# Norm2 and the gate operands by token quarters inside the output projection; down weights first, and first and last down pairs with the inner tile outermost

## The chip, the cores and the metric

The kernel runs on one core of one Trainium2 chip. Its engines are TensorE (PE, matmuls; PEld is its weight load), VectorE (DVE), ScalarE (ACT), GpSimd (POOL) and SyncE (SP), whose queue issues every DMA of this kernel. The metric is the device time of one execution in microseconds, the median of the runs of a kernel. A profile is one execution; its span goes from the first to the last instruction.

## The reference

One encoder layer, for a prompt of 1024 tokens and a sample of 32, which the kernel holds side by side as T = 1056 columns. What matters here is its second half:

```python
    m = jax.nn.sigmoid(ga_br) * y_a + jax.nn.sigmoid(gb_br) * y_b
    x = x + gate1 * (m @ w_out)

    h2 = _rms_norm(x, norm2_g) * (1 + scale2) + shift2
    g, up = jnp.split(h2 @ w_gate_up, 2, axis=-1)
    x = x + gate2 * ((jax.nn.silu(g) * up) @ w_down)
```

All is float32. D_MODEL is 1024 (8 tiles of 128), D_FF is 2816 (22 tiles). The shifts, scales and gates come from a conditioning vector, one for the prompt and one for the sample.

## The kernel before

**Precision.** Each float32 operand is split in two parts that TensorE takes: `split` (L81 to L83) writes a rounded copy (the high part, an ACT cast, L82) and the difference to it (the low part, a subtraction on VectorE, L83). A product is three matmuls: high by high, high by low, low by high.

**Output projection (L885 to L907).** `m` lies in `oh` and `ol`, all 1056 columns. For each of the 8 output tiles `n`, `wpiece` loads 512 KB of weights through a staging buffer `st` (`stage`, two buffers, shared by all loads of this half) and splits them into two of the seven `ws` buffers. `out_unit` (L818) runs 24 matmuls into one of six PSUM buffers `u`, adds gate and residual on VectorE (L815), and adds the square to `ssq` (ACT L829, DVE L830). The residual itself comes by `residual_in` (L786): a load through `st`, eight transposes on PE into a PSUM buffer `x` (two of them), two copies. The tiles 0 to 4 run over three groups of 352 columns. The last three have their weights held, and run over four quarters of QW = 264 columns: first quarters 0 and 2 for each tile, then 1 and 3.

**Norm2 and operands.** Gate and up projection use a Strassen scheme with seven products. It is run for two token groups: group 0 pairs quarters 0 and 2, group 1 quarters 1 and 3. `norm2(g)` (L832) sums the squares over the partitions with 128x1 matmuls (L839), takes the power -1/2 (DVE L841, POOL L842), spreads the result over the partitions with matmuls against the identity (L850), multiplies (DVE L854) and modulates (ACT L857). This gives four blocks of 4 x 264 columns per group, b11, b12 (both upper four tiles; first and second quarter) and b21, b22. `operands` (L863) forms from them, in place, B11, T1 = b12 - b11, T2 = b22 - T1, T3 = b22 - b12, B22, T4 = b21 - T2 and B21, each split in two; the low part of B21 on POOL. `norm2(0)` starts behind the second of the six last output units, its second part behind the fourth; `operands(0)` stands behind the last unit.

**Gate-up (L1019 to L1049).** Per pair of tiles `f0` and for gate (`uw` 0) and up (`uw` 1), `wstrassen` forms seven weight operands, which fill the seven `ws` buffers, and `strassen` (L951) runs seven products of 12 matmuls per group. They take the operands in the order B11, T2, T1, B21, T3, B22, T4 (`SEQ`, L917). The first gate pass is run for group 0 alone, with `norm2(1)` hooked in behind its products 1 and 4; then comes `operands(1)`, then the same pass for group 1. All other passes run both groups. The result of each tile is stored to `a_d`. The 14 operands lie in three places: four in `Ta`, free from the start; eight in `Tb`, where `oh` and `ol` were; two in the place of `xb`.

**Down projection (L1053 to L1138).** The 22 tiles of the inner dimension are taken in two halves of 11 (`KC`). `a_load` (L991) brings one tile of `a_d` through `st` and splits it into one of 11 places: two (`k0`, `k1`) loaded early, nine where the Strassen operands were, which come free as the last gate-up pass moves on. Three more places (`late`) take the first three tiles of the second half. `x1_load` brings the residual `x1` back, eight loads of 528 KB. `d_piece` loads the weights of one output tile, 1408 rows, in two loads, and fills three `ws` buffers. In each half the output tiles 0 and 1 are a pair with the inner tile outermost: 18 matmuls per inner tile into six PSUM buffers. Tiles 2 to 5 follow one by one, then 6 and 7, three column groups each. Behind the first half the eight places left are loaded anew. In the second half the outputs are transposed and stored on the way.

**What sets the order.** PE runs in the order of the lines. The order on ACT, DVE, POOL and SP is made when the kernel is built, by a scheduler that knows the dependencies and the buffers; each engine then runs its own queue strictly in that order, and a waiting instruction holds up what is queued behind it. So a DMA of x1 (L909) can stand in the middle of the output projection though its line is behind it.

Of the kernel before, what the change touches and what calls it, by code (L numbers as in the profile page):

```python
# [7 lines left out]
F32 = mybir.dt.float32  # L8
# [30 lines left out]
def hybrid_layer(tc, x_prompt, x_sample, cache_k, cache_v, state_conv, c_prompt, c_sample,  # L39
# [726 lines left out]
    OPS = ("B11", "T1", "T2", "B21", "T3", "B22", "T4")  # L766
# [10 lines left out]
    Ta = sb("Ta", side="right")  # L777
    Dp = sb("Dp", side="right")
# [53 lines left out]
    def norm2(g):  # L832

        qs = (g * QW, g * QW + HW)
        starts = (0, P, QW - P)
        pm = x_tile()
        for j, q in enumerate(qs):
            for i, c in enumerate(starts):
                pe.matmul(pm[:, 3 * j + i:3 * j + i + 1], ssq[:, q + c:q + c + P], ones[:, 0:1], start=True, stop=True)  # L839
        rs = Dp.tile([P, 6], F32, tag="rs2", name="rs2", bufs=2)  # L840
        dve.tensor_scalar(out=rs, in0=pm[:, 0:6], scalar1=EPS, scalar2=None, op0=ALU.add)  # L841
        pool.tensor_tensor(out=rs, in0=rs, in1=mhalf[:, :6], op=ALU.pow)  # L842

        def rest():
            b = {}
            for j, q in enumerate(qs):
                pr = x_tile()
                for i, c in enumerate(starts):
                    c0 = i * P - c
                    pe.matmul(pr[:, c + c0:c + P], rs[:, 3 * j + i:3 * j + i + 1].to_broadcast([P, P]), ident[:, c0:],  # L850
                              start=True, stop=True)
                for i, x in enumerate((xa, xb)):
                    h2 = Dq.tile([P, 4, QW], F32, tag=f"h2{i}{j}", name="h2", bufs=1)
                    dve.tensor_mul(h2, x[:, :, q:q + QW], pr[:, :QW].unsqueeze(1).to_broadcast([P, 4, QW]))  # L854
                    for n in range(4):
                        for c0, c1, s in pieces(q, QW):
                            act.activation(h2[:, n, c0:c1], h2[:, n, c0:c1], AF.Identity,  # L857
                                           scale=a2[:, 4 * i + n, s:s + 1], bias=mod[:, 3 * KT + 4 * i + n, s:s + 1])
                    b[i, j] = h2
            return b  # L860
        return rest

    def operands(g, b):  # L863

        def parts(o, src, eng=dve):
            split(src, Top[o, g][:, 0], Top[o, g][:, 1], eng)

        b11, b12, b21, b22 = b[0, 0], b[0, 1], b[1, 0], b[1, 1]
        parts("B11", b11)
        dve.tensor_sub(b11, b12, b11)  # L870
        t1 = b11
        parts("B22", b22)
        dve.tensor_sub(b12, b22, b12)
        t3 = b12
        dve.tensor_sub(b22, b22, t1)
        t2 = b22
        parts("T2", t2)
        parts("T1", t1)
        parts("B21", b21, pool)
        dve.tensor_sub(b21, b21, t2)  # L880
        t4 = b21
        parts("T3", t3)
        parts("T4", t4)

    for n in range(KT - 3):  # L885
# [8 lines left out]
    LAST = tuple(range(KT - 3, KT))  # L894
    w3 = [wpiece(wo_v[:, :, n * P:(n + 1) * P]) for n in LAST]
    alloc_ops(Ta, order[:NTA])
    for n, w_ in zip(LAST, w3):
        for j, q in enumerate((0, 2)):
            out_unit(n, w_, q * QW, QW, (lambda n=n: residual_in(n)) if j == 0 else None)
    todo = [(n, w_, q) for n, w_ in zip(LAST, w3) for q in (1, 3)]  # L900
    blocks = []
    for i, (n, w_, q) in enumerate(todo):
        out_unit(n, w_, q * QW, QW)
        if i == 1:
            stat = norm2(0)
        if i == 3:
            blocks.append(stat())  # L907
# [259 lines left out]
```

## Time and profile before

| | |
|---|---|
| median of 3 runs | 2210.89 us (2209.64 to 2211.85) |
| the profiled execution | 2211.65 us |
| its span | 2209.9 us |
| mean granted TensorE clock | 0.970 |
| PE busy | 2066.9 us (94%) |
| DVE, ACT, POOL busy | 1218.1, 771.9, 391.3 us |
| DMA | 206.93 MB, mean 94 GB/s |

Every matmul record has a length that overlaps the next one, so PE's time is read from counts per stretch and from the idle times before a group of matmuls. An arrow "<-" names what ended an idle time: the engine and line, or the DMA, that released it. PEclk is the clock that was granted to TensorE, as a share of full speed. In the text the stretches of the span are given in microseconds from its start: the output projection ends at 1386.5, the gate-up stage at 1883.6, the first half of the down projection at 2042.

### The profile page before, as it was taken

To read this page: it belongs to the slowest core of one execution; us is meant where nothing else is said; L and a number is where in the kernel's file an instruction comes from. 1 tells how busy PE (TensorE), PEld (TensorE's weight loads), DVE (VectorE), ACT (ScalarE), POOL (GpSimd) and SP (SyncE) were. 2 spreads that over 40 slices of the span, in tenths; PEclk is the share of its full clock that TensorE was granted. 3 is DMA by queue.
4 is the path that set the end of the run, shared out by engine and by line. 5 is a ranking of instruction groups with operands and counts; after the bars stand their busy time and mean duration, and the time that the engine had idled before them with its cause. 6 is when DMAs were issued, how large, how long until landed. Compare 5 with 4: busy or idle time off the path is not lost.

```text
span 2209.9 us, 36054 instructions
## 1 busy us (share of the span) xinstructions
PE 2066.9 (94%) x13931; PEld 2018.9 (91%) x13931; DVE 1218.1 (55%) x2770; ACT 771.9 (35%) x1875; POOL 391.3 (18%) x644
## 2 busy tenths in 40 slices
PE   7899999999999999999999999589999999599699
PEld 5899998989999999999999999489999999599598
DVE  5665656565656556555576845665555555222232
ACT  5354545444444444322221222633333333111210
POOL 2333333333333232000000000111211211000000
PEclk9999999999999999999999999689999999799799
DMA  9211212021212010546586533112322324512321
GB/s 263 76 55 49 67 38 79 21 82 30 75 30 73 28 45 17 148 155 186 164 258 200 166 97 118 37 59 78 94 72 74 92 69 119 189 40 79 104 67 55
DMA packets 286195, 206.93 MB, mean 94 GB/s; under 512 B 12976, under 2 KB 269768, under 8 KB 286024
## 3 DMA queue, kind: packets, MB, share of 16 engines
q1 hardware_dynamic: 286024, 204.63, 30.6%
q8 instruction: 110, 1.80, 0.3%
q14 instruction: 61, 0.50, 0.1%
HBM read 153.74 MB, written 50.84 MB: 93 GB/s over the span
## 4 chain that ended last, share of the span: by engine, by line
PE 59%; DVE 3%; DMA 3%; ACT 2%; issue 1%; POOL 1%; SPq 0%; ACTq 0%; DVEq 0%; POOLq 0%
PE u L970 17%; PE u L689 7%; PE u L687 7%; PE u L688 7%; PE u L1087 4%; PE u L1089 4%; PE u L1088 4%; DMA st<-a_d 1%; PE mm L526 1%; DMA st<-in_w_down_dram 1%; PE mm L527 1%; PE mm L528 1%; PE mm L485 1%; PE mm L487 1%; PE mm L486 1%
## 5 line engine op out<-in xcount | busy, mean ns | idle before, releaser
L82 ACT CAST ws<-st 128x512 fp32r<-128x512 f32 (+1 forms) x282 | 170.5, 614 | 503.8 <-PE u L1089 122.8
L83 DVE TENSOR_TENSOR ws<-st,ws 128x512 fp32r<-128x512 f32 (+1 forms) x260 | 181.5, 704 | 293.9 <-ACT ws L82 292.3
L970 PE MATMUL u<-T,ws 128*128 128x264 f32 x1848 | 240.7, 287 | 19.6 <-ACT T L82 14.7
L970 PEld LDWEIGHTS u<-T,ws 128*128 128x128 f32 x1848 | 232.9, 191 | 21.1 <-ACT T L82 15.3
L1087 PE MATMUL u<-ka,ws 128*128 128x352 f32 x480 | 159.4, 332 | 49.9 <-ACT ws L82 49.9
L526 PE MATMUL mm<-hh,wh 128*128 128x352 f32 x576 | 198.4, 344 | 0.0
L970 PE MATMUL u<-B,ws 128*128 128x264 f32 x1320 | 174.7, 286 | 15.5 <-ACT B L82 14.1
L528 PE MATMUL mm<-hh,wl 128*128 128x352 f32 x576 | 188.1, 327 | 0.0
L527 PE MATMUL mm<-hl,wh 128*128 128x352 f32 x576 | 187.9, 326 | 0.0
L485 PE MATMUL mm<-qh,hh 128*128 128x384 f32 x512 | 183.8, 359 | 3.0 <-ACT hh L82 2.9
L970 PEld LDWEIGHTS u<-B,ws 128*128 128x128 f32 x1320 | 167.1, 190 | 16.6 <-ACT B L82 14.5
L487 PE MATMUL mm<-qh,hl 128*128 128x384 f32 x512 | 174.0, 340 | 0.0
L486 PE MATMUL mm<-ql,hh 128*128 128x384 f32 x512 | 173.2, 338 | 0.0
L1089 PE MATMUL u<-ka,ws 128*128 128x352 f32 x480 | 157.7, 328 | 0.1
L1088 PE MATMUL u<-ka,ws 128*128 128x352 f32 x480 | 156.9, 327 | 0.0
L414 ACT ACTIVATE p<-S,nmx,rs 128x128 f32<-128x128 f32 (+5 forms) x144 | 113.3, 789 | 117.2 <-DVE nmx L410 76.5
L1087 PEld LDWEIGHTS u<-ka,ws 128*128 128x128 f32 x480 | 92.2, 192 | 51.3 <-ACT ws L82 51.3
L242 DVE SCALAR_TENSOR_TENSOR adacc<-adw,sc,adacc 128x128 f32<-128x128 f32 x448 | 130.2, 346 | 0.6
L687 PE MATMUL u<-oh,ws 128*128 128x352 f32 (+1 forms) x408 | 129.7, 318 | 0.0
L689 PE MATMUL u<-oh,ws 128*128 128x352 f32 (+1 forms) x408 | 127.9, 313 | 0.0
L688 PE MATMUL u<-ol,ws 128*128 128x352 f32 (+1 forms) x408 | 127.6, 313 | 0.0
L687 PE MATMUL u<-hh,ws 128*128 128x352 f32 x384 | 125.9, 328 | 0.0
(252 smaller groups left out, 4775.9 us busy)
## 6 DMA issues: line engine op xcount, KB each, us to landing
st<-in_w_gate_up_dram SPq DMA_DIRECT2D x44, 512.0 KB, 3.8
adw<-in_w_ada_dram SPq DMA_DIRECT2D x43, 512.0 KB, 4.5
st<-in_w_in_dram SPq DMA_DIRECT2D x40, 512.0 KB, 4.2
qst<-in_w_in_dram SPq DMA_DIRECT2D x24, 512.0 KB, 4.7
st<-a_d SPq DMA_DIRECT2D x22, 528.0 KB, 3.6
a_d<-xa SPq DMA_DIRECT2D x84, 132.0 KB, 2.0
st<-in_w_down_dram SPq DMA_DIRECT2D x16, 512.0 KB, 4.3
z_d<-z SPq DMA_DIRECT2D x24, 176.0 KB, 2.6
```

The lines of the kernel that those rows point to most:

```text
L485: pe.matmul(pj[:, 0:384], a, qh[:, :, kt, :], start=kt == 0, stop=False)
L487: pe.matmul(pj[:, 0:384], b, qh[:, :, kt, :], start=False, stop=kt == KT - 1)
L526: pe.matmul(pt[:, :gw], wh[:, kt, :], hh[:, kt, g0:g0 + gw], start=kt == 0, stop=False)
L527: pe.matmul(pt[:, :gw], wh[:, kt, :], hl[:, kt, g0:g0 + gw], start=False, stop=False)
L528: pe.matmul(pt[:, :gw], wl[:, kt, :], hh[:, kt, g0:g0 + gw], start=False, stop=kt == KT - 1)
L687: pe.matmul(pt[:, :gw], wh, ah[:, kt, g0:g0 + gw], start=kt == 0, stop=False)
L688: pe.matmul(pt[:, :gw], wh, al[:, kt, g0:g0 + gw], start=False, stop=False)
L689: pe.matmul(pt[:, :gw], wl, ah[:, kt, g0:g0 + gw], start=False, stop=kt == KT - 1)
L970: pe.matmul(q[dst], l, t[:, r, j, :], start=first and j == n == 0, stop=j == 3 and n == 2, skip_group_check=not first)
L1087: pe.matmul(pt[:, :gw], wh, ah, start=kt == 0, stop=False)
L1088: pe.matmul(pt[:, :gw], wh, al, start=False, stop=False)
L1089: pe.matmul(pt[:, :gw], wl, ah, start=False, stop=kt == KC - 1)
```

## The change

Three things are changed.

- *Output projection.* Four output tiles are held instead of three (the first of them in a buffer `wx` of its own), and the quarter is the outer loop: quarters 0, 2, 1, 3, each over tiles 4 to 7. Norm2 is taken apart by quarters (`stats`, `spread`, `h2_block`), and its parts and those of `operands` are put between the units: for quarters 0 and 2 behind units of quarters 2 and 1, the start of quarter 1 behind units of quarter 3. What is left of group 0 (T3, B22, T4) and the rest of quarter 1 follow behind the last unit; quarter 3 is hooked into the first gate pass behind its products 1 and 3. B21 goes to `Ta` with B11, T1 and T2 as before, and its low part to VectorE.
- *Loads of the down projection.* The weights of the first pair stand ahead of the activations, and the activations have one staging buffer `sa` of their own instead of the two of `st`.
- *Down projection.* The last pair of the first half, too, has the inner tile outermost, and behind each inner tile the place that comes free is loaded anew. The three `late` loads stand behind the weights of tile 2.

```diff
-    OPS = ("B11", "T1", "T2", "B21", "T3", "B22", "T4")
+    OPS = ("B11", "B21", "T1", "T2", "T3", "B22", "T4")
...
+    starts = (0, P, QW - P)
+
+    def stats(q):
+
         pm = x_tile()
...
+        for i, c in enumerate(starts):
+            pe.matmul(pm[:, i:i + 1], ssq[:, q * QW + c:q * QW + c + P], ones[:, 0:1], start=True, stop=True)
+        rs = Dp.tile([P, 3], F32, tag="rs2", name="rs2", bufs=2)
+        dve.tensor_scalar(out=rs, in0=pm[:, 0:3], scalar1=EPS, scalar2=None, op0=ALU.add)
+        pool.tensor_tensor(out=rs, in0=rs, in1=mhalf[:, :3], op=ALU.pow)
+        return rs
+
+    def spread(rs):
+
+        pr = x_tile()
+        for i, c in enumerate(starts):
+            c0 = i * P - c
+            pe.matmul(pr[:, c + c0:c + P], rs[:, i:i + 1].to_broadcast([P, P]), ident[:, c0:], start=True, stop=True)
+        return pr
+
+    def h2_block(pr, q, i):
+
+        h2 = Dq.tile([P, 4, QW], F32, tag=f"h2{i}{q // 2}", name="h2", bufs=1)
+        dve.tensor_mul(h2, (xa, xb)[i][:, :, q * QW:(q + 1) * QW],
+                       pr[:, :QW].unsqueeze(1).to_broadcast([P, 4, QW]))
+        for n in range(4):
+            for c0, c1, s in pieces(q * QW, QW):
+                act.activation(h2[:, n, c0:c1], h2[:, n, c0:c1], AF.Identity,
+                               scale=a2[:, 4 * i + n, s:s + 1], bias=mod[:, 3 * KT + 4 * i + n, s:s + 1])
+        return h2
...
+    def first(q, g):
+
+        pr = spread(box[q])
+        box[1, 1] = h2_block(pr, q, 0)
+        op_parts("B11", g, box[1, 1])
+        box[2, 1] = h2_block(pr, q, 1)
+        op_parts("B21", g, box[2, 1])
+
+    def g0_second():
+        pr = spread(box[2])
+        b11, b21 = box[1, 1], box[2, 1]
+        b12 = h2_block(pr, 2, 0)
         dve.tensor_sub(b11, b12, b11)
+        op_parts("T1", 0, b11)
+        b22 = h2_block(pr, 2, 1)
+        dve.tensor_sub(b11, b22, b11)
+        op_parts("T2", 0, b11)
+        dve.tensor_sub(b21, b21, b11)
         dve.tensor_sub(b12, b22, b12)
+        box["t"] = b12, b22, b21
+
+    def g0_third():
+        for o, src in zip(("T3", "B22", "T4"), box["t"]):
+            op_parts(o, 0, src)
+
+    def g1_first():
+        box["pr"] = spread(box[1])
+        box[1, 1] = h2_block(box["pr"], 1, 0)
+
+    def g1_second():
+        op_parts("B11", 1, box[1, 1])
+        box[2, 1] = h2_block(box["pr"], 1, 1)
+        op_parts("B21", 1, box[2, 1])
+
+    def g1_third():
+        pr = spread(box[3])
+        c11 = box[1, 1]
+        c12 = h2_block(pr, 3, 0)
+        dve.tensor_sub(c11, c12, c11)
+        op_parts("T1", 1, c11)
+        box["t"] = c12, h2_block(pr, 3, 1)
+
+    def g1_fourth():
+        c11, c21 = box[1, 1], box[2, 1]
+        c12, c22 = box["t"]
+        dve.tensor_sub(c11, c22, c11)
+        op_parts("T2", 1, c11)
+        dve.tensor_sub(c12, c22, c12)
+        op_parts("T3", 1, c12)
+        op_parts("B22", 1, c22)
+        dve.tensor_sub(c21, c21, c11)
+        op_parts("T4", 1, c21)
...
+    HELD = 4
+    for n in range(KT - HELD):
...
+    held = [[wx[:, :, 0:4], wx[:, :, 4:8]]] + [wpiece(wo_v[:, :, n * P:(n + 1) * P]) for n in LAST[1:]]
     alloc_ops(Ta, order[:NTA])
...
+    after = {(2, 0): lambda: stat(0), (2, 2): lambda: first(0, 0), (1, 0): lambda: stat(2), (1, 2): g0_second,
+             (3, 0): lambda: stat(1), (3, 2): g1_first}
+    for q in (0, 2, 1, 3):
+        for i, (n, w_) in enumerate(zip(LAST, held)):
+            out_unit(n, w_, q * QW, QW, (lambda n=n: residual_in(n)) if q == 0 else None)
+            if (q, i) in after:
+                after[q, i]()
...
-    operands(0, blocks[0])
+    g0_third()
+    g1_second()
...
-        st = stage()
+        st = Ep.tile([P, T], F32, tag="sa", name="sa", bufs=1)
         sp.dma_start(st, a_d[kt])
...
                 if k == 1:
-                    box.append(norm2(1))
-                if k == 4:
-                    box.append(box[0]())
+                    stat(3)
+                if k == 3:
+                    g1_third()
...
-            operands(1, box[1])
+            g1_fourth()
...
+    first_w = [d_piece(0, n) for n in (0, 1)]
+    keys = [("k0",), ("k1",), ("B11", 0), ("B11", 1), ("T2", 0), ("T2", 1), ("T1", 0), ("T1", 1), ("B21", 0),
+            ("B21", 1), ("T3", 0)]
+    for kt in range(2, KC):
+        ahl.append(a_load(kt, slot(keys[kt])))
...
+    def d_pair(ws2, n0, after=None):
+
         pts = [u_tile() for _ in range(6)]
         for kt in range(KC):
             for i in range(2):
                 for gi, (g0, gw) in enumerate(GROUPS):
                     d_mm(pts[3 * i + gi], ws2[i], kt, g0, gw)
+            if after:
+                after(kt)
...
+    def reload(kt):
+
+        if len(nxt) < KC:
+            key = keys[kt]
+            t = slot(key) if len(key) > 1 else Ep.tile([P, 2, T], F32R, tag=key[0], name="ka")
+            nxt.append(a_load(KC + len(nxt), t))
+
+    d_pair(first_w, 0)
+    for n in range(2, KT - 2):
+        w = d_piece(0, n)
+        if n == 2:
+            nxt += [a_load(KC + i, t) for i, t in enumerate(late)]
+        for g0, gw in GROUPS:
+            d_unit(w, n, g0, gw)
+    ws2 = [d_piece(0, n) for n in (KT - 2, KT - 1)]
+    first_w = []
+    d_pair(ws2, KT - 2, reload)
+    ahl = nxt
+    d_pair([d_piece(1, n) for n in (0, 1)], 0)
...
```

More of the change, by code (lines that the diff above doesn't have):

```diff
@@ L830, in out_unit @@
             dve.tensor_add(ssq[:, g0:g0 + gw], ssq[:, g0:g0 + gw], sq)
-    def norm2(g):
-        qs = (g * QW, g * QW + HW)
-        starts = (0, P, QW - P)
+    starts = (0, P, QW - P)
+    def stats(q):
         pm = x_tile()
[L837 to L883, printed above, removed]
@@ L885, in hybrid_layer @@
-    for n in range(KT - 3):
+        for i, c in enumerate(starts):
[10 more added lines that the diff above has]
+        return pr
@@ L1057, in slot, with d_piece @@
         return home[key].tile([P, 2, T], F32R, tag=f"{key[0]}{key[1]}", name="ka")
-    for i, key in enumerate((("B11", 0), ("B11", 1), ("T2", 0), ("T2", 1), ("T1", 0), ("T1", 1), ("B21", 0),
-                             ("B21", 1), ("T3", 0))):
-        ahl.append(a_load(2 + i, slot(key)))
+    def d_piece(c, n):
+        out = []
+        for k0, k1 in ((0, 8), (8, KC)):
+            v = stage()[:, :(k1 - k0) * P].rearrange("p (a b) -> p a b", b=P)
+            sp.dma_start(v, wdn_v[:, c * KC + k0:c * KC + k1, n * P:(n + 1) * P])
+            out += wsplit(v)
+        return out
+    first_w = [d_piece(0, n) for n in (0, 1)]
[3 more added lines that the diff above has]
+        ahl.append(a_load(kt, slot(keys[kt])))
     F = sb("F")
@@ L1106, in out_tiles @@
             sp.dma_start(dst[:, k0 * P:k0 * P + 512], yt[:n])
-    for c in range(2):
-        ws2 = [d_piece(c, n) for n in (0, 1)]
+    def d_pair(ws2, n0, after=None):
         pts = [u_tile() for _ in range(6)]
@@ L1124, in hybrid_layer @@
-        ws2 = [d_piece(c, n) for n in (KT - 2, KT - 1)]
-        for gi, (g0, gw) in enumerate(GROUPS):
-            for i in range(2):
-                d_unit(ws2[i], KT - 2 + i, g0, gw)
-                if c and gi and not i:
-                    out_tiles(((0, 1), (2, 3, 4))[gi - 1], 4)
-        if c == 0:
-            ahl = [a_load(KC + i, t) for i, t in enumerate(late)]
-            for i, key in enumerate((("k0",), ("k1",), ("B11", 0), ("B11", 1), ("T2", 0), ("T2", 1), ("T1", 0),
-                                     ("T1", 1))):
-                t = slot(key) if len(key) > 1 else Ep.tile([P, 2, T], F32R, tag=key[0], name="ka")
-                ahl.append(a_load(KC + len(late) + i, t))
+                residual(x1n[n0 + i], pts[3 * i + gi], n0 + i, g0, gw, 5)
@@ new lines, in hybrid_layer @@
+    first_w = []
+    d_pair(ws2, KT - 2, reload)
+    ahl = nxt
+    d_pair([d_piece(1, n) for n in (0, 1)], 0)
+    for n in range(2, KT - 2):
+        w = d_piece(1, n)
+        for gi, (g0, gw) in enumerate(GROUPS):
+            d_unit(w, n, g0, gw)
+            if n >= 4:
+                out_tiles((((0, 1), (2, 3), (4,)), ((5,), (6, 7), (8,)))[n - 4][gi], 0)
+    ws2 = [d_piece(1, n) for n in (KT - 2, KT - 1)]
+    for gi, (g0, gw) in enumerate(GROUPS):
+        for i in range(2):
+            d_unit(ws2[i], KT - 2 + i, g0, gw)
+            if gi and not i:
+                out_tiles(((0, 1), (2, 3, 4))[gi - 1], 4)
```

41 lines of the change are left out of this document (13 added, 28 removed).

## The prediction

> **What bounds the kernel now.** First the page: who is busy.
>
> ```profile
> span 2209.9 us, 36054 instructions
> PE 2066.9 (94%) x13931; PEld 2018.9 (91%) x13931; DVE 1218.1 (55%) x2770; ACT 771.9 (35%) x1875; POOL 391.3 (18%) x644
> ```
>
> TensorE (PE) is the bound, and only its idle time and its slow stretches can be won. Then the waits of PE over the run, longest sums first (us, times, longest):
>
> ```profile
> PE u L1087 <- ACT ws L82: 49.9, 4, 23.3
> ...
> PE u L970 <- ACT T L82: 14.7, 2, 8.1
> PE u L970 <- ACT B L82: 14.1, 2, 9.7
> PE u L970 <- DVE T L83: 3.6, 2, 1.8
> ...
> PE u L970 <- DVE B L83: 1.4, 2, 0.7
> PE u L970 <- DVE t L986: 1.3, 1, 1.3
> ```
>
> All of these lie where the diff is: the first two Strassen half-passes of the gate-up stage (L970) and the two starts of the down projection (L1087). Busy time by stretch shows what each place costs with the clock:
>
> ```profile
> core 0: us, PE busy (x) PEld busy (x) DVE busy (x) ACT busy (x) POOL busy (x), PEclk, DMA share, GB/s
> 1346.00:1386.50 40.50, 40.50 (x338) 40.30 (x336) 24.04 (x44) 15.64 (x32) 1.74 (x1) 1.00 0.28 93
> 1386.50:1454.50 68.00, 34.14 (x195) 32.10 (x195) 46.16 (x50) 37.01 (x64) 9.13 (x4) 0.65 0.08 24
> 1500.00:1800.00 300.00, 300.00 (x2479) 300.00 (x2478) 168.18 (x314) 92.91 (x187) 55.91 (x61) 1.00 0.26 79
> 1883.60:2042.00 158.40, 131.95 (x793) 130.83 (x792) 41.03 (x66) 22.24 (x33) 2.14 (x3) 0.90 0.30 96
> 1925.00:2035.00 110.00, 110.00 (x686) 110.00 (x685) 27.52 (x48) 13.09 (x20) 0.00 (x0) 1.00 0.19 58
> 2042.00:2138.20 96.20, 72.63 (x430) 71.54 (x430) 27.12 (x43) 17.17 (x25) 0.00 (x0) 0.88 0.27 83
> ```
> ```profile
> 1386.50:1454.50 68.00, 30.82 (x170) 28.36 (x171) 0.65 0.08 24
> ```
>
> The last row is the second window again, for L970 alone. Undisturbed, a 264-column matmul takes 300/2479 = 0.121 us and a 352-column one 110/686 = 0.160. So the loss is
>
> - place 1, from the end of the output projection (E = 1386.5) to the end of the second half-pass: 68.0 - 170 x 0.121 - about 2.5 for 25 small matmuls = 44.9 us, of which 33.8 are waits (14.7 + 14.1 + 3.6 + 1.4) and 11 the clock of 0.65;
> - place 2, from the last gate-up matmul to the end of the first half of the down projection: 158.4 - 793 x 0.160 = 31.3;
> - place 3, its second half up to the first output transpose: 96.2 - 430 x 0.160 = 27.3;
> - the 1.3 of L986.
>
> Together 104.8. The profiled execution took 2211.65 for a span of 2209.9 (1.75 lie around it), 0.8 above the median of 2210.89. With all of this gone it would take 2106.9, and the change adds no PE work (16 output units of 264 columns stand for 12 of 264 and three of 352, 0.4 us). The forecast is this floor plus what is left or new.
>
> **Place 1: norm2 and the operands.** PE's timeline shows what it waits for:
>
> ```profile
> 1390.98 0.59 PE L970 MATMUL u<-B,ws 128*128 128x264 f32 x1 [4.47 <-ACT B L82]
> ...
> 1403.19 0.59 PE L970 MATMUL u<-T,ws 128*128 128x264 f32 x1 [8.13 <-ACT T L82]
> ...
> 1441.26 0.59 PE L970 MATMUL u<-T,ws 128*128 128x264 f32 x1 [6.58 <-ACT T L82]
> 1443.66 0.59 PE L970 MATMUL u<-T,ws 128*128 128x264 f32 x1 [1.81 <-DVE T L83]
> ```
>
> Twice, for token group 0 and for group 1, it waits for B11 (the longer of these two waits was 9.7, above) and then for T2. The work behind it, in the timelines of ScalarE and VectorE and grouped by line for 1386 to 1455:
>
> ```profile
> 1381.25 8.10 ACT L857 ACTIVATE h<-h,mod,a 128x264 f32<-128x264 f32 x16 [0.72 <-DVE h L854]
> ...
> 1418.65 10.31 ACT L857 ACTIVATE h<-h,mod,a 128x264 f32<-128x264 f32 x24 [1.03 <-DVE h L854]
> ```
> ```profile
> 1417.30 1.26 DVE L854 TENSOR_TENSOR h<-xa,x 128x1056 f32<-128x1056 f32 x1
> ```
>
> ```profile
> L83 DVE TENSOR_TENSOR T<-h,T 128x1056 fp32r<-128x1056 f32 x7 | 8.7, 1249 | 0.0
> L82 ACT CAST T<-h 128x1056 fp32r<-128x1056 f32 x7 | 7.5, 1072 | 11.8 <-DVE h L870 7.0 <-DVE h L875 2.1 <-DVE h L873 1.5
> L870 DVE TENSOR_TENSOR h<-h,h 128x1056 f32<-128x1056 f32 x2 | 7.1, 3548 | 0.0
> L83 DVE TENSOR_TENSOR ws<-st,ws 128x512 fp32r<-128x512 f32 x8 | 6.5, 817 | 0.7 <-ACT ws L82 0.7
> L83 POOL TENSOR_TENSOR B<-h,B 128x1056 fp32r<-128x1056 f32 x2 | 5.6, 2782 | 37.7 <-ACT B L82 37.7
> L873 DVE TENSOR_TENSOR h<-h,h 128x1056 f32<-128x1056 f32 x2 | 2.5, 1252 | 0.0
> L977 DVE TENSOR_TENSOR u<-u,p 128x264 f32<-128x264 f32 x2 | 0.9, 432 | 2.2 <-PE u L970 2.2
> ```
>
> Per group there are 4 products by the norm, 4 differences and 7 low parts, 1.25 us each; before, one low part ran on POOL. There L870, of the same shape as L873, took 3.55 beside the POOL subtraction of 2.78. Taking that off POOL saves VectorE 2.3 and costs it 1.25: -1 per group.
>
> Group 0: 12 of its VectorE operations (products, differences, B11, B21, T1, T2) now lie inside the output projection, 12 x 1.25 = 15 us. The first window shows cover: VectorE 24.04 of 40.5 us busy, 16.5 free, and ScalarE 24.9 free for 8.1 (16 activations) + 4 x 1.07 = 12.4. It fits just so; where it overflows, E slips by the overflow. On PE the matmuls that spread the norm stand two units behind those that sum it, 48 x 0.121 = 5.8 us of cover for VectorE's and POOL's step between; without it the output units queue behind that step. POOL's queue loses its two long subtractions and has four short powers for two. The three operands left (T3, B22, T4) need the space of the projection's inputs, so they start at E, 3 x 1.25 = 3.8, and PE needs T3 only after 48 x 0.121 = 5.8. The waits of 4.47 and 8.13 go.
>
> Group 1: its T2 stays late. Behind E VectorE still has two differences and three low parts of group 0; for group 1 four products, two differences and the low parts of B11, B21, T1 and T2: 5 + 10 = 15 x 1.25 = 18.8; four weight low parts, 4 x 0.7 (0.82 beside POOL); five pass sums and the last residual, 5 x 0.43 + 1. That is 24.8, or about 24 since they follow each other slightly closer. PE reaches T2 after 84 + 12 matmuls of 0.121 and 1.5 of small ones, 13.1 after E. So it waits 11, with the rest of group 1's pass and the next weights' pass queued behind, and about 3 more go to the clock (11 in the two rounds before): **14 left**. From below: the bare chain behind the hook at 5.8 is product, 8 activations at 10.31 / 24 = 0.43, difference, cast, low part, difference, cast, low part, 11.8 long, ends at 17.6 and leaves 5 + 2 = 7. From above: before, the same chain took from 1417.2 to 1443.7, 26; then 19 + 5 = 24. I take 14, since VectorE's queue rather than the chain sets the end.
>
> The queues passed: four residual loads now stand one unit (2.9 us) apart plus transposes instead of two units, through two stage buffers that also bring the held weights:
>
> ```profile
> st<-in_x_prompt_dram SPq DMA_DIRECT2D x8, 512.0 KB, 5.2
> ```
>
> A load of 5.2 per buffer pair every 3.9 just keeps up; a miss costs up to 5. I take 1 (0 to 5). The eight stores of x1 move on SP from between the units to behind E for four of them; gate-up weights behind them are wanted only a whole pass later.
>
> **Places 2 and 3: the down projection.** PE's longest wait, one reload cycle of a staging buffer in the chain of waits, and the transfers of the two kinds that share the queue (KB, us to landing):
>
> ```profile
> 1906.91 0.66 PE L1087 MATMUL u<-ka,ws 128*128 128x352 f32 x1 [23.25 <-ACT ws L82]
> ```
> ```profile
> 1895.35 10.81 DMA st<-in_w_down_dram
> ...
> 2037.36 1.08 ACT ka L82
> 2038.46 1.27 DVE ka L83
> 2039.75 3.36 DMA st<-a_d
> 2043.19 1.08 ACT ka L82
> ```
> ```profile
> st<-in_w_down_dram SPq DMA_DIRECT2D x16, 512.0 KB, 4.3
> ...
> ka<-x_d SPq DMA_DIRECT2D x4, 528.0 KB, 6.3
> ```
>
> The weights come last, behind nine activation loads in the same two buffers. Now they go first: three pieces in each of two weights, whose buffers come free one by one in the last gate-up pass, so they are ready at 1883.6. The activations get a buffer "sa" of their own, but only one: 2043.19 - 2037.36 = 5.83 us per load where two buffers gave about 2.9. The first down pair has the inner tile outermost already before; a step takes 18 x 0.160 = 2.89. Tile 2's place (B11, both groups) is free after 12 matmuls of the last gate-up pass, 1883.6 - 168 x 0.121 + 1.5 = 1864.8, its split done 1.08 + 1.27 later, near 1867.4; tile 10 is ready at 1867.4 + 8 x 5.83 = 1914.0, wanted at 1883.6 + 28.9 = 1912.5: wait 1.5. But eight loads of x1, 528 KB each, fall into the same 20 us. Behind them the weight load of 1895.35 took 10.81 instead of 4.3: +6.5. **I take one such delay, 8 left**; none gives 2, two give 15. If the order of SP's queue brought the weights last again, all 31 would stay.
>
> The Trainium skill ("Trainium Kernel Development and Optimization", Best Practices) asks for double buffers so that loads overlap compute; the one "sa" buffer goes against it. By it, two buffers would leave 0 at place 2 and make it 2123; this trace agrees as far as 5.83 exceeds the 2.89 of a step.
>
> Place 3: eight loads into places that come free one per step in the last pair of the first half (now inner tile outermost): load j ready at 2.89 + 2.4 + 5.83 j after that pair's start, for j = 7 at 46.1; wanted at 31.8 + 10 x 2.89 = 60.7. The cover is 14.6 us of PE work; three more tiles come earlier. Of the next weights, the first fits the seventh buffer, the rest follow after steps 4 and 8. **1 left** (0 to 6, one weight load and its split).
>
> The Trainium skill ("TensorE: Matmul & The Clock Gate", Why this matters for your kernels) says that a PE idle gap over some 3 us brings half clock; the 0.65 agrees. By it the leftover at place 2 would cost about 3 more if it came as one gap.
>
> Sum: 2106.9 + 14 + 1 + 8 + 1 = **2131 us**, 80 less.
>
> **Rivals.**
> - *Nearly all is won*: chain bound at place 1, x1 loads out of the way: 2106.9 + 7 + 2 = 2116. For it: DMA share only 0.30 in place 2. Against: VectorE's 24 us.
> - *One place stays*: the order of ScalarE, VectorE and SP is made when the kernel is built, not by the lines, and the operands of group 1 come as late as before (24), E slips or residual loads miss (5), two delays at place 2 (15), 4 at place 3: 2155. For it: VectorE's free 16.5 against 15.
> - *The single buffer takes over and it gets slower*: if every load waits like the one at 1895.35, a cycle is 10.81 + 1.08 + 1.27 = 13.2. Place 2 then ends 1867.4 + 8 x 13.2 - 1912.5 = 60 late, place 3 5.3 + 7 x 13.2 - 60.7 = 37 late: 2106.9 + 14 + 1 + 60 + 37 = 2219. It decides from 15 p - 100.5 = 90, a cycle p of 12.7. Against it: 3.36 with 0.27 DMA share.
> - *It doesn't do what it says*: the builder orders the weights behind the activations again and VectorE makes up place 1's gain as a later E: 2211.
>
> **How the numbers follow.** Forecast 0.55, nearly all 0.15, one place stays 0.25, slower 0.04, no change 0.01. The likeliest's own range is 2118 to 2145. For 8 in 10 it reaches halfway into both neighbours and takes the bounds in: 2113 to 2162. A difference under 0.2% (4.4 us) can't be told from none; faster 0.94, same 0.02, slower 0.04.
>
> **What would show it.** PE's waits: L1087's 49.9 falls under 10, split over steps that wait for ka, not ws; one wait of some 10 us before the second operand of group 1, none for B at group 0; no idle PE around the middle of the down projection; the granted clock at 0.98 or more. Wrong would be: x or residual waits of PE inside the output projection, ka loads further apart than 6 us, or a wait on ws at either start.

## The result and the profile after

| | before | after |
|---|---|---|
| median of 4 runs each, same chip | 2211.37 us (2209.64 to 2211.96) | 2148.32 us (2145.98 to 2150.82) |
| ratio, 95% interval | | 0.9716 (0.9699 to 0.9733) |
| profiled execution, span | 2211.65, 2209.9 us | 2149.89, 2148.1 us |

The change makes the kernel 63 us faster, where 80 were forecast. The page of the kernel after, span and busy time:

```profile
span 2148.1 us, 36100 instructions
...
PE 2060.6 (96%) x13955; PEld 2014.5 (94%) x13955; DVE 1215.7 (57%) x2775; ACT 770.8 (36%) x1875; POOL 384.8 (18%) x644
```

PE is busy 6 us less though it runs 24 matmuls more: less of its work falls into half clock (the mean granted clock is 0.987 where it was 0.970). The waits of PE over the whole run (us, times, longest), those of the changed places:

```profile
PE x L839 <- DVE ssq L831: 6.9, 3, 4.5
...
PE u L1013 <- ACT T L82: 6.5, 1, 6.5
...
PE x L850 <- POOL rs L842: 3.0, 1, 3.0
...
PE x L794 <- DMA st<-in_x_prompt_dram: 2.8, 2, 2.5
```

The 49.9 us for weights of the down projection and the waits for B operands are gone. The first row and the last two are new: they lie in and right behind the output projection. To see what each place won, both traces are cut at the same six points: the first residual transpose of the output projection, its last unit (E), the end of the second half-pass, the last gate-up matmul, the end of the first half of the down projection, and the first output transpose. The busy time by stretch (its length, busy times, PEclk, DMA share, GB/s), the output projection before and then all five after:

```profile
1287.30:1386.40 99.10, 99.10 (x722) 98.65 (x720) 49.67 (x92) 31.95 (x63) 1.74 (x1) 1.00 0.39 124
```
```profile
1290.10:1403.20 113.10, 104.32 (x759) 103.07 (x757) 61.71 (x106) 40.66 (x76) 3.52 (x3) 0.97 0.35 109
1403.20:1440.00 36.80, 24.90 (x182) 23.78 (x181) 30.45 (x39) 27.00 (x50) 2.14 (x2) 0.86 0.14 44
1440.00:1867.40 427.40, 427.40 (x3531) 427.40 (x3530) 241.16 (x447) 138.14 (x277) 80.31 (x86) 1.00 0.29 88
1867.40:2005.20 137.80, 132.31 (x794) 130.48 (x793) 44.37 (x66) 28.19 (x38) 1.01 (x2) 0.98 0.42 133
2005.20:2076.40 71.20, 69.45 (x432) 69.17 (x432) 21.10 (x38) 10.67 (x16) 0.00 (x0) 1.00 0.22 66
```

| stretch | before | after | won | forecast to win |
|---|---|---|---|---|
| head, unchanged code | 1287.3 | 1290.1 | -2.8 | 0 |
| output projection to E | 99.1 | 113.1 | **-14.0** | -1 |
| E to the end of the second half-pass | 67.8 | 36.8 | 31.0 | 30.9 |
| rest of gate-up | 429.3 | 427.4 | 1.9 | 1.3 |
| first half of the down projection | 158.3 | 137.8 | 20.5 | 23.3 |
| second half to the first output transpose | 96.4 | 71.2 | 25.2 | 26.3 |
| sum, span | | | 61.8 | 80.8 |

Of the 19.0 us that are missing, 13.0 lie in one row: the output projection got 14 us longer, where 1 was forecast.

**Where the 14 us are.** PE's timeline of the kernel after, the rows that stand behind an idle time (start, us, instruction, idle time and what ended it):

```profile
1372.72 0.80 PE L839 MATMUL x<-ones,ssq 128*128 128x1 f32 x6 [1.39 <-DVE ssq L831]
...
1390.52 1.41 PE L839 MATMUL x<-ones,ssq 128*128 128x1 f32 x6 [4.49 <-DVE ssq L831]
...
1414.34 0.83 PE L850 MATMUL x<-ident,rs 128*128 128x128 f32 x6 [3.00 <-POOL rs L842]
1427.70 0.59 PE L1013 MATMUL u<-T,ws 128*128 128x264 f32 x1 [6.50 <-ACT T L82]
```

The first two rows are the sums of squares of quarters 2 and 1, inside the output projection. They take six tiny matmuls, but the output units stand behind them in PE's queue. The second of them needs the square of the last unit of quarter 1. Its way leads from VectorE (residual, L816) over ScalarE (square, L830) back to VectorE (add, L831):

```profile
1383.12 0.49 DVE L816 SCALAR_TENSOR_TENSOR xb<-u,mod,xb 128x264 f32<-128x264 f32 x1 [0.28 <-PE u L689]
1383.57 1.26 DVE L881 TENSOR_TENSOR h<-h,h 128x1056 f32<-128x1056 f32 x1
1386.07 0.46 DVE L816 SCALAR_TENSOR_TENSOR xb<-u,mod,xb 128x232 f32<-128x232 f32 x1 [1.24 <-PE u L689]
1386.44 1.25 DVE L83 TENSOR_TENSOR T<-h,T 128x1056 fp32r<-128x1056 f32 x1
1387.61 1.25 DVE L887 TENSOR_TENSOR h<-h,h 128x1056 f32<-128x1056 f32 x1
1388.78 1.25 DVE L884 TENSOR_TENSOR h<-h,h 128x1056 f32<-128x1056 f32 x1
1389.95 0.43 DVE L831 TENSOR_TENSOR ssq<-ssq,sq 128x264 f32<-128x264 f32 x1
```
```profile
1381.43 3.60 ACT L860 ACTIVATE h<-h,mod,a 128x264 f32<-128x264 f32 x7 [0.90 <-DVE h L856]
1384.94 1.06 ACT L82 CAST T<-h 128x1056 fp32r<-128x1056 f32 x1
1385.90 0.60 ACT L860 ACTIVATE h<-h,mod,a 128x264 f32<-128x264 f32 x1
1386.41 0.41 ACT L830 ACTIVATE sq<-xb 128x264 f32<-128x264 f32 x1
```

The residual was done at 1383.61, but the square began only at 1386.41: ScalarE's queue had seven modulations, a cast and an eighth modulation of group 0 ahead of it. The square was ready at 1386.82. The 0.43 us that add it to `ssq` began at 1389.95, behind three operand steps of group 0 of 1.25 us each, none of which PE wanted yet. So PE idles 4.49 us, of which VectorE's three steps are 3.13 and ScalarE's queue the rest. The 1.39 us of quarter 2 are ScalarE's alone: there the residual was done at 1368.93, the square began at 1371.70, again behind modulations and a cast, and the add followed it at once, at 1372.14. VectorE is not full: in the stretch 1290.1 to 1403.2 it is busy 61.7 of 113.1 us, and ScalarE 40.7. Short steps that release PE stand behind long ones in queues whose order is fixed. The idle time also brings half clock:

```profile
1390.52:1396.10 5.58, 5.58 (x26) 5.58 (x27) 3.49 (x6) 1.66 (x3) 0.85 (x1) 0.50 0.24 97
```

The 14.0 us come apart as 5.9 for the sums (1.39 + 4.49), 2.8 for residual loads, and 5.2 of more PE busy time (104.32 - 99.10), of which half clock is 5.58 / 2 = 2.8; the last 2.4 are one more round of sums and of spreads (0.80 + 0.73), 0.1 for the split units (4 x 24 x 0.121 less 3 x 24 x 0.160), and 0.8 not taken apart.

**Place 2.** The casts of the nine activation tiles in ScalarE's timeline, and PE's gaps in the first pair:

```profile
1849.04 1.08 ACT L82 CAST ka<-sa 128x1056 fp32r<-128x1056 f32 x1
...
1861.27 1.07 ACT L82 CAST ka<-sa 128x1056 fp32r<-128x1056 f32 x1 [1.73 <-DMA sa<-a_d]
1869.87 1.07 ACT L82 CAST ka<-sa 128x1056 fp32r<-128x1056 f32 x1 [4.62 <-DMA sa<-a_d]
1876.47 1.07 ACT L82 CAST ka<-sa 128x1056 fp32r<-128x1056 f32 x1 [5.53 <-DMA sa<-a_d]
1885.61 1.08 ACT L82 CAST ka<-sa 128x1056 fp32r<-128x1056 f32 x1 [8.06 <-DMA sa<-a_d]
...
1904.44 1.08 ACT L82 CAST ka<-sa 128x1056 fp32r<-128x1056 f32 x1 [4.72 <-DMA sa<-a_d]
```
```profile
1893.04 0.42 PE L1130 MATMUL u<-ka,ws 128*128 128x352 f32 x1 [2.00 <-ACT ka L82]
1894.33 0.62 PE L1131 MATMUL u<-ka,ws 128*128 128x352 f32 x1 [0.87 <-DVE ka L83]
```

Two cycles are long, 8.6 (1861.27 to 1869.87) and 9.1 (1876.47 to 1885.61); all eight take 55.4 where 8 x 5.83 + 6.5 = 53.1 were forecast. The stretch lost 137.8 - 793 x 0.160 = 10.9 to waits and clock, 8 were forecast.

### The profile page after: what moved, and what is told of

It is laid out like the page before. It is cut to its first block, busy times and chain, and to the rows that moved or that the text cites. A ratio compares the mean times of both kernels' runs of the same rounds, so it can differ in the third digit from the quotient of the medians.

```text
span 2148.1 us, 36100 instructions
## 1 busy us (share of the span) xinstructions
PE 2060.6 (96%) x13955; PEld 2014.5 (94%) x13955; DVE 1215.7 (57%) x2775; ACT 770.8 (36%) x1875; POOL 384.8 (18%) x644
## 5 line engine op out<-in xcount | busy, mean ns | idle before, releaser
L687 PE MATMUL u<-hh,ws 128*128 128x352 f32 x384 | 125.9, 328 | 0.0
L689 PE MATMUL u<-hh,ws 128*128 128x352 f32 x384 | 124.9, 325 | 0.0
L688 PE MATMUL u<-hl,ws 128*128 128x352 f32 x384 | 124.2, 323 | 0.0
L687 PE MATMUL u<-oh,ws 128*128 128x352 f32 (+1 forms) x384 | 123.2, 321 | 0.0
L689 PE MATMUL u<-oh,ws 128*128 128x352 f32 (+1 forms) x384 | 121.0, 315 | 0.0
```

The lines of the kernel that those rows point to most:

```text
L687: pe.matmul(pt[:, :gw], wh, ah[:, kt, g0:g0 + gw], start=kt == 0, stop=False)
L689: pe.matmul(pt[:, :gw], wl, ah[:, kt, g0:g0 + gw], start=False, stop=kt == KT - 1)
```

## The experiments

The head, whose code no kernel here changes, ended between 1285.7 and 1292.4 in the profiled executions. Most kernels below were executed once. So they are compared by the stretches behind the head, and by times only where there are four executions of each, in turn on one chip. The kernel before took 2210.71 us beside the single executions.

The stretches vary too. The kernel after was profiled a second time (it is the kernel "after, again" of the last table); its output projection and the stretch from E to the end of the second half-pass:

```profile
1289.40:1402.10 112.70, 104.45 (x758) 103.35 (x757) 61.77 (x106) 40.62 (x76) 3.52 (x3) 0.97 0.35 109
1402.10:1441.70 39.60, 28.36 (x181) 27.31 (x180) 30.39 (x39) 27.11 (x50) 2.14 (x2) 0.78 0.13 41
```

Together they take 152.3 us, where the first execution took 149.9, because more of the second stretch ran at half clock (0.78 for 0.86); the waits for `ssq` are 6.9 and that for the spread 3.0 in both. The first half of the down projection took 136.0 (1869.1 to 2005.1) instead of 137.8. So a difference under some 2.5 us in a stretch is not clear. PE's idle time, the length less the busy time, varies less: 20.7 and 19.5 us up to the end of the second half-pass.

### Each half of the change alone

The down projection's part on the kernel before (diff against before, its core):

```diff
-        st = stage()
+        st = Ep.tile([P, T], F32, tag="sa", name="sa", bufs=1)
         sp.dma_start(st, a_d[kt])
...
+    first_w = [d_piece(0, n) for n in (0, 1)]
...
+    d_pair(first_w, 0)
...
+    d_pair(ws2, KT - 2, reload)
```

> The kernel before with the down projection of the changed one (weights first, own staging buffer, both pairs with the inner tile outermost), and norm2 and the operands left as they were. By the split of the two traces the norm2 part won 31 us in the first gate passes and gave 14 back in the output projection, 17 net, so this kernel should take 2148 + 17 = 2165 us (2161 to 2169), with the output projection ending near 1386 to 1389 and 11 us left at the start of the down projection. If instead the 30 us of the forecast had been won and some other stage had lost 13, it should take about 2178.

And the norm part on the kernel before:

```diff
+    HELD = 4
+    for n in range(KT - HELD):
...
+    for q in (0, 2, 1, 3):
+        for i, (n, w_) in enumerate(zip(LAST, held)):
...
+    g0_third()
+    g1_second()
```

> The kernel before with norm2 and the operands of the changed one, and the down projection left as it was. If the parts add up: 2211 - 17 = 2194 us (2190 to 2198), the output projection again ending some 14 us later than before, with PE waits for ssq of about 7 and for residual loads of about 3. If the late end of the output projection came from anything in the new order of loads of the down projection (SBUF places, the queue of SP), it goes here, and the time is 2181.

Measured: 2162.36 and 2196.7 us, both as expected. The windows of the first (output projection, then the two stretches of the down projection), and the output projection of the second:

```profile
1285.70:1384.70 99.00, 99.00 (x722) 98.63 (x719) 49.58 (x92) 31.88 (x63) 1.74 (x1) 1.00 0.39 124
1881.60:2019.40 137.80, 131.56 (x793) 129.67 (x792) 44.97 (x67) 28.48 (x38) 1.64 (x3) 0.98 0.43 137
2019.40:2088.90 69.50, 69.50 (x433) 69.27 (x432) 20.66 (x37) 10.66 (x16) 0.00 (x0) 1.00 0.20 61
```
```profile
1289.60:1402.60 113.00, 106.07 (x758) 104.84 (x756) 61.86 (x106) 40.81 (x76) 3.52 (x3) 0.95 0.35 109
```

The parts win 48.4 and 14.0, together 62.4, as much as the whole: if they touch each other, it is by less than executions differ. The 14 us of the output projection belong to the norm part alone (113.0 against 99.0), and most of what the whole wins is the down projection's. The residual loads cost the norm part 0.8 instead of the 3 expected; more half clock (0.95 for 0.97) made its output projection as long all the same.

### Sums of squares later, or on another engine

If the sums' place in PE's queue is the cause, a second unit of cover ahead of them takes the slip away. The sums and what follows move one unit back, and the two hooks in the gate pass one product back:

```diff
-    after = {(2, 0): lambda: stat(0), (2, 2): lambda: first(0, 0), (1, 0): lambda: stat(2), (1, 2): g0_second,
-             (3, 0): lambda: stat(1), (3, 2): g1_first}
+    after = {(2, 0): lambda: stat(0), (2, 2): lambda: first(0, 0), (1, 1): lambda: stat(2), (1, 3): g0_second,
+             (3, 1): lambda: stat(1), (3, 3): g1_first}
...
-                if k == 1:
+                if k == 2:
                     stat(3)
-                if k == 3:
+                if k == 4:
                     g1_third()
```

> The changed kernel with the sums of squares of quarters 2, 1 and 3 on PE, and what follows them, one unit (or one product) later. Theory (PE stands in its queue at the sum's matmuls, since the last add to ssq is queued on VectorE behind long operand subtractions): the waits of 1.4 and 4.5 fall under 1 each, the half clock inside the output projection goes, its end comes 7 to 9 us earlier, the operands of group 1 come at most 3 later: 2139 to 2144 us. Rival (VectorE as a whole is too full, and the wait only moves to T2 of group 1): the end comes earlier but T2's wait grows by as much, 2146 to 2150.

Measured: 2148.63 us. Its windows up to E and behind it, and PE's waits there:

```profile
1290.10:1394.20 104.10, 101.83 (x751) 101.05 (x749) 55.05 (x95) 36.56 (x68) 1.72 (x2) 0.98 0.35 108
1394.20:1440.60 46.40, 27.82 (x187) 26.76 (x187) 35.46 (x50) 30.46 (x56) 2.96 (x3) 0.82 0.17 58
```
```profile
PE u L1013 <- ACT ws L82: 9.1, 1, 9.1
PE u L1013 <- ACT T L82: 6.8, 1, 6.8
```

No wait for `ssq` is left, and the output projection takes 104.1 instead of 113.1. So the sums' place is shown as the cause of 9.0 of the 14.0 us (0.7 of them are only moved: the spread of quarter 1 now runs behind E). But the stretch behind takes 46.4 instead of 36.8, and nothing is won in sum. PE is now so early that it waits 9.1 us for the first gate weights, whose splits stand behind the operand steps on ScalarE and VectorE. A gain was expected, or, by the rival, a longer wait for T2. The time is the rival's, but the new wait came at the weights; those for T2's two parts grew only from 7.8 to 8.5 together.

The other way leaves the places and gives the adds of the last four output tiles to POOL:

```diff
-            dve.tensor_add(ssq[:, g0:g0 + gw], ssq[:, g0:g0 + gw], sq)
+            (pool if n >= KT - 4 else dve).tensor_add(ssq[:, g0:g0 + gw], ssq[:, g0:g0 + gw], sq)
```

> The changed kernel with the adds to ssq of the last four output tiles on GpSimd instead of VectorE, so that they are queued behind no operand work. Theory: PE's wait for ssq falls from 6.9 to under 3 in all and the end of the output projection comes 4 to 8 us earlier: 2140 to 2145. Rival (the residual's multiply-add on VectorE is as late as the add, or GpSimd and VectorE hold each other up): the wait stays above 5, 2147 to 2153.

Measured: 2151.73 us. PE's waits in the same stretches:

```profile
PE x L839 <- POOL ssq L831: 4.4, 3, 2.3
PE u L1013 <- ACT ws L82: 3.7, 1, 3.7
```

The sums wait less (4.4 for 6.9), which lies between the expectation (under 3) and the rival (above 5). What is left of it is ScalarE's queue: the square of quarter 1's last unit begins at 1386.02, again 2.8 us behind its residual, and POOL's add follows at 1386.57. E comes 112.9 behind the first residual transpose, as before this edit, since more half clock (0.95 for 0.97) took what the waits gave. The stretch behind it grows to 43.6 from 36.8 (39.6 in the second execution) with two new waits for weights (this one, and 2.6 on VectorE's part of the split). The time is in the rival's range. So taking the add off VectorE is not enough; what stands between it and PE is the order of two queues.

### The first gate weights ahead of the leftover operands

On top of the later sums, the lines that load and split the first gate weights go ahead of `g0_third` and `g1_second`:

```diff
+    w0 = gu_w(0, 0)
     g0_third()
     g1_second()
...
-        w = gu_w(f0, 0)
+        w = gu_w(f0, 0) if f0 else w0
```

> The kernel with the sums one unit later, and the first gate weights' splits traced ahead of the operands that are left (T3, B22, T4 of group 0, B11 and B21 of group 1) instead of behind them. Theory (the 9.1 us wait for ws that came in place of the waits for ssq is an order made at build, by the place in the lines, and not a lack of VectorE or ScalarE time, which are busy 47 and 42 of 65 us): that wait falls under 1, the first gate pass runs through and the wait for T2 of group 1 grows by less than 4: 2140 to 2145 us. Rival (the two engines' work is too much for the place, and a wait only moves): the wait for T2 grows by 6 or more, 2146 to 2150.

Measured: 2138.57 us. From the first residual transpose to the end of the second half-pass it takes 144.3 (102.9 + 41.4), against 149.9 after and 150.5 with the later sums alone: 5.6 won, of which 4.3 are idle time of PE (16.4 for 20.7). 3.3 more of its time is the head. The waits:

```profile
PE u L1017 <- ACT T L82: 7.1, 1, 7.1
PE u L1017 <- ACT ws L82: 3.3, 1, 3.3
```

The wait for weights fell from 9.1 to 3.3, with 1.0 more for VectorE's part of the split; under 1 was expected. The one for T2 of group 1 did not move. Whether that one is set by the chain behind quarter 3's norm or by the queues was asked by putting the hooks back to products 1 and 3:

```diff
-                if k == 2:
+                if k == 1:
                     stat(3)
-                if k == 4:
+                if k == 3:
                     g1_third()
```

> The kernel before this one with the two hooks of quarter 3 back behind products 1 and 3 of the first pass. If T2 of group 1 is set by the chain behind quarter 3's norm, it comes up to 2.9 us earlier: 2 to 3 us less than the kernel before this one. If it is set by the queue of operand work ahead of it on VectorE and ScalarE: no less, and PE waits for ssq or the power instead.

Measured: 2143.48 us, and 146.3 from the first residual transpose to the end of the second half-pass. The 2.0 more are not clear, and PE's idle time is 15.9 for 16.4. T2 waits 6.9 us, but the edit did not do what it was to do. PE ran the sums of quarter 3 1.8 us earlier (10.7 behind E instead of 12.6), yet VectorE took their result up at the same place of its queue (L841, 14.5 behind E instead of 14.4), and the spread even came 0.8 later. So the question stays open by this run. What it does show is that VectorE's queue sets when that chain starts. The wait for `ssq` or the power that was expected in that case did not come either.

The kernel after shows how T2 goes on from there:

```profile
1413.21 0.15 DVE L841 TENSOR_SCALAR rs<-x 128x3 f32<-128x3 f32 x1
...
1415.21 1.25 DVE L856 TENSOR_TENSOR h<-xa,x 128x1056 f32<-128x1056 f32 x1 [1.38 <-PE x L850]
...
1423.24 1.26 DVE L83 TENSOR_TENSOR T<-h,T 128x1056 fp32r<-128x1056 f32 x1 [1.26 <-ACT T L82]
```

The sums ended at 1408.1, and VectorE came to them at 1413.21, 5 us later, behind operand steps. From the product of quarter 3 at 1415.21 to T2 at 1427.70 it is 12.5 us, and in that time VectorE waits for ScalarE, which has 16 modulations for quarter 3 (6.5 us) where another quarter has 8, since its last 32 columns are the sample's and are modulated apart. So VectorE's queue delays the start of the chain, and ScalarE paces what follows.

### The single buffer and the x1 loads

Two causes were in question for the 10.9 us at place 2. A second whole buffer for the activations was not run; instead they come in halves of 528 columns through three half buffers, half as much space more:

```diff
-        st = Ep.tile([P, T], F32, tag="sa", name="sa", bufs=1)
-        sp.dma_start(st, a_d[kt])
-        split(st, t[:, 0], t[:, 1])
+        for c in (0, HW):
+            st = Ep.tile([P, HW], F32, tag="sa", name="sa", bufs=3)
+            sp.dma_start(st, a_d[kt, :, c:c + HW])
+            split(st, t[:, 0, c:c + HW], t[:, 1, c:c + HW])
```

> The changed kernel with each activation load of the down projection in two halves of 528 columns through three staging buffers of half the size, instead of one of full size. Theory (the single buffer makes cycles of 5.8 us and more, over the 2.9 that a step of PE takes): the stretch from the last gate-up matmul to the end of the first half falls from 137.8 us to 129 to 132, PE's waits for ka there under 2, in all 2139 to 2144 us. Rival (the transfers of x1 and the weights fill the DMA engines, whatever the buffers): the stretch stays over 135, 2146 to 2150.

And the loads of x1 are taken out (its places are filled with zeros, which leaves the residual out of the layer's output):

```diff
-            sp.dma_start(t[:, i], x1_d[k0 + i])
+            pool.memset(t[:, i], 0.0)
```

> The changed kernel without the eight loads of x1 (4.3 MB) ahead of the down projection: their places are filled with zeros by GpSimd, so that the second residual is left out of the output. Theory (the x1 transfers lengthen two reload cycles of the single buffer, from about 6 to 8.6 and 9.1 us): all cycles at 5.8 to 6.5, the stretch of 137.8 falls to 130 to 133, in all 2141 to 2145 us. Rival (the buffer alone, or the weight loads of the next output tiles, set it): two cycles stay over 8, 2147 to 2150.

Measured: 2139.73 and 2141.72 us. The windows of the first half of the down projection, halves first:

```profile
1867.10:1996.80 129.70, 128.03 (x794) 127.39 (x793) 48.30 (x84) 31.07 (x54) 2.09 (x3) 1.00 0.45 145
```
```profile
1862.10:1997.60 135.50, 131.42 (x794) 130.18 (x793) 45.40 (x67) 27.90 (x38) 7.09 (x8) 0.97 0.35 105
```

With halves the stretch falls from 137.8 to 129.7, and no wait for an activation is left. The run doesn't separate what the number of buffers does from what the smaller pieces do. Without the x1 loads it falls to 135.5 only, less than expected: the cycle of 9.1 is gone, the one of 8.6 is still there with 8.7 (casts at 1861.66 and 1870.40). In the kernel after that load was issued 2 us after its buffer came free, behind stores of the last gate-up results in SP's queue. So x1 is at most 2.3 of the 10.9, and against the 136.0 of the second execution only 0.5, which is not clear. The single buffer, which lets every delay through, is the main part. The first expectation held; the second was too large for the stretch, and its time fell into the expected range only because the head was 4.4 shorter.

The Trainium skill ("Trainium Kernel Development and Optimization", Best Practices) asks to double-buffer so that DMA overlaps compute. These runs agree, with 8.1 us (6.3 against the second execution).

### Both, and one more order

The weights ahead and the halves together, executed four times, in turn with the kernel after itself on the same chip (before: 2210.79 us):

```diff
+    w0 = gu_w(0, 0)
     g0_third()
...
+        for c in (0, HW):
+            st = Ep.tile([P, HW], F32, tag="sa", name="sa", bufs=3)
```

> The sums one unit later, the first gate weights ahead of the operands left, and the activation loads in halves through three buffers, together. If the two places are independent, their gains over the changed kernel add: about 6 and 10 less, 2148 - 16 = 2132 us (2129 to 2136). If the loads of one hold up the other, 2137 or more.

> The changed kernel itself, unaltered, in the same rounds as the two ahead of it, so that they are compared on one chip: 2146 to 2151 us.

The same with T2 taken fourth in group 1's first pass, behind B21 instead of ahead of T1:

```diff
-    def strassen(w, gs, dest, epi, hook=None):
+    def strassen(w, gs, dest, epi, hook=None, seq=SEQ):
...
-        for k, (wo_, to_, dst) in enumerate(SEQ):
+        for k, (wo_, to_, dst) in enumerate(seq):
```

> The kernel before this one with another order of the products in the first pass of group 1: B11, T1, B21, T2 instead of B11, T2, T1, B21. Theory (T2 comes at a time that the queues of VectorE and ScalarE set, whatever PE does): 24 more matmuls of 0.121 us stand ahead of T2, so its wait falls from about 8.7 by 2.9, and the clock stays higher after it: 3 to 5 us less. Rival (T1 or B21 come as late as T2, and the wait moves to them): no less.

| kernel | median of 4 runs (range) | ratio to before (95%) |
|---|---|---|
| after, again | 2147.65 (2142.75 to 2149.81) | 0.9708 (0.9692 to 0.9724) |
| weights ahead and halves | 2133.82 (2132.24 to 2134.92) | 0.9652 (0.9637 to 0.9666) |
| and T2 fourth | 2133.90 (2131.64 to 2137.40) | 0.9654 (0.9640 to 0.9668) |

The two edits add: 13.8 us off the kernel after, where the stretches gave 5.6 + 8.1. The version beats both kernels, and its range and that of the kernel after don't meet. With T2 fourth, the wait for a T operand that ScalarE casts is this:

```profile
PE u L1017 <- ACT T L82: 2.9, 1, 2.9
```

T2's 7.1 are gone; T1, now ahead of it, waits 2.9, and B21 waits 1.4 for the copy of the first product. From the first residual transpose to the end of the second half-pass it is 143.2 against 145.5, with 12.8 us of idle time for 16.4, but the times don't tell the two kernels apart, where 3 to 5 us less were expected.

## Why the prediction was right and wrong

- **The floor, the losses and what gets rid of them: right.** Of 104.8 us of losses named before, the three places and L986 won 31.0 + 20.5 + 25.2 + 1.9 = 78.6. The waits for B11, for T2 of group 0 and for down weights went as worked out.
- **"It fits just so; where it overflows, E slips by the overflow": the step that failed.** The sum took 1 for the output projection, and it slipped by 14.0. VectorE did have the time (it is busy 61.7 of 113.1 us), so there was no overflow; the question was the wrong one. It fitted even better than the prediction reckoned, since the four products of group 0 (L854, 1379.96 to 1385.05 on VectorE in the kernel before) were already in the 24.04 us of its window: VectorE's busy time there grew by 12.0, not 15. The prediction gave cover to the step behind the sums, two units or 5.8 us, and that step made PE wait only once, behind E. It gave none to the steps ahead of them: the sums stand one unit (24 x 0.121 = 2.9 us) behind their quarter's last unit, and need ScalarE's last square and VectorE's last add, which the queues may put behind any number of operand steps. With two units of cover the waits for `ssq` are gone, as the later sums show. It was named among the signs of being wrong (waits of PE inside the output projection), but priced only at 5, together with the residual loads, in the rival "one place stays". The 0.4 us for the units of 264 columns come out as 0.1.
- **Place 1's rest, 14 left: right in sum, partly by luck.** E to the end of the second half-pass took 36.8; less 168 x 0.121 and 2.5 of small matmuls, 14.0 are left (16.8 in the second execution). Of the waits behind it T2 is 7.8 (6.50 and 1.34), not 11; the sums of quarter 3 (1.06) and their spread (3.00) are the rest. T2 came near the time that was forecast, its high part 24.5 us and its low part 26.4 behind E for "about 24", but PE came to it at 18.0 instead of 13.1, held up by the sums and the spread. That 24 was so near is luck too. VectorE's 24.8 counted two differences of group 0 (T3 at 1387.61, T4 at 1390.29) and a product of group 1 (1400.37) that ran ahead of E; in their place VectorE stood idle 4.8 us behind E, for casts, the spread and modulations. And the bare chain took 8 activations for quarter 3, which has 16. So "VectorE's queue rather than the chain" holds for the start of the chain only.
- **Residual loads, 1 (0 to 5): 2.8.** The size was off, inside its bounds (0.8 to 2.8 in the kernels that have the norm part). What would take it away was not tried.
- **Place 2, 8 (2 to 15): 10.9.** The mechanism was right, a cycle of one buffer with a delay behind x1; the second delay, behind the stores of the gate-up results, was not seen. The one was priced at 6.5 and the two are 9.1 - 5.83 = 3.3 and 8.6 - 5.83 = 2.8, so the sum was near because two errors offset. Two whole buffers, which were to leave 0, were not run; three halves left 129.7 - 126.9 = 2.8.
- **Place 3, 1: 71.2 - 430 x 0.160 = 2.4.** No wait for `ka` or weights in that stretch, but 1.7 us for PSUM buffers that VectorE had to empty at the end of the pair with the inner tile outermost, which the forecast left out; the down part alone took 69.5.
- **The head**, taken as equal, was 2.8 later in the profiled execution; that is no effect of the change.

By the table, the misses are 13.0 in the output projection (1.8 of them the loads), 2.8 and 1.1 in the two halves of the down projection and 2.8 in the head, less 0.7 in gate-up: 19.0, and the profiled execution took 2149.9 against 2131. Of the rivals, "one place stays" named the kind of miss ("E slips or residual loads miss") at 5 us; the single buffer did not take over, since no cycle came near 12.7. The measured 2148.3 lies in the 2113 to 2162 that were given for 8 in 10, but above the 2118 to 2145 of the likeliest outcome. Two of the signs of being wrong came: waits inside the output projection, and `ka` loads further apart than 6 us.

**Open:** the waits left in the best version, 7.1 + 1.7 for T2, 3.2 + 0.7 for the first gate weights and 2.7 for residual loads; and whether an order of VectorE's queue exists that feeds both the sums and the weights in time.

## What to carry to other kernels

When work is moved beside a busy PE, ask of every instruction that PE itself must run for it (here six tiny matmuls) how far it stands behind the step it reads, and what the other engines' queues may put between; free time of those engines is no answer. A wait that is removed uncovers the next one in the same queue, so what feeds PE next has to be moved up in the same edit. A staging buffer of which there is one passes every delay of the load queue on; three halves in one and a half times the space left 2.8 us, where two whole ones were expected to leave none.

## What was not expected of the hardware

**Half clock without a long gap.** Four windows of 3.4 us around the two gaps at 1893 shown above, in the kernel after; the third number from the end of a line is the granted clock:

```profile
1891.00:1894.40 3.40, 0.54 (x3) 0.26 (x2) 2.17 (x4) 1.49 (x2) 0.00 (x0) 1.00 0.54 164
1894.40:1897.80 3.40, 3.40 (x12) 3.40 (x13) 1.50 (x3) 1.14 (x2) 0.00 (x0) 0.50 0.80 243
1897.80:1901.20 3.40, 1.64 (x9) 1.11 (x8) 1.40 (x2) 1.07 (x1) 0.00 (x0) 1.00 0.56 164
1901.20:1904.60 3.40, 3.40 (x12) 3.40 (x13) 0.00 (x0) 0.16 (x1) 0.00 (x0) 0.50 0.48 163
```

No gap was longer than 2.00 us, yet a window in which PE was busy 0.54 of 3.40 us, and one with 1.64, were each followed by 3.4 us at half clock. The Trainium skill ("TensorE: Matmul & The Clock Gate", Why this matters for your kernels) warns of PE idle gaps over some 3 us between bursts; here several shorter ones within one window did it, so the measurement decides. The rows fit a rule that goes by the idle share of such a window; they don't show it, nor how large the share would have to be. The same page of the Trainium skill (Part 1, What's actually happening) gives the window as about 3.4 us and running freely; the two stretches of half clock, 3.4 us long and 6.8 apart, agree. And the same wait can go either way: behind the 3.00 us for the spread of quarter 3 the next 12 matmuls took 1.70 us in one execution of the kernel after and 2.99 in the other.

**The head varies.** The same code up to the first residual transpose took 1285.7 us in the down part alone and 1292.4 in the kernel with T2 fourth. In the busy time of these two stretches PE has 1231.76 and 1238.54 us: its busy time grows by 6.8 us, its idle time does not. What sets it is not shown. A single execution can therefore not tell kernels apart that differ by less than about 7 us; the four of the kernel after, again, lie 7.1 apart.
